# A two-layer hybrid decoder on one core: z chunks between the SSD's halves, SSD groups in three spaced steps, a later norm sum, LRU squares on ScalarE

## The chip, the cores and the metric

The kernel runs on one NeuronCore of a Trainium2 chip. The metric is the device time of one execution in microseconds (us), taken as the median of several runs. The engines are called TensorE (PE in the profile, with PEld for its weight loads), VectorE (DVE), ScalarE (ACT), GpSimd (POOL) and SyncE (SP, which issues nearly all DMAs here).

## The reference, cut to what matters

A trunk of two layers over 256 tokens of width 1024, all in float32. Each layer normalizes and modulates `x`, multiplies it by one wide `w_in`, and feeds three mixers from the product: dilated attention (`q`, `k`, `v`), a Mamba-2 state space mixer (`z`, `xbc`, `dt`; here "SSD"), and a gated linear recurrence ("LRU"). Their outputs are merged under sigmoid gates. A mixture of 32 experts follows.

```python
def mixer_block(h, ...):
    proj = h @ w_in
    q, k, v, z, xbc, dt_raw, lru_gate, lru_x, merge = jnp.split(proj, cuts, axis=-1)
    ...
    y_ssd = ssd_mixer(z, xbc, dt_raw, ...)
    y_lru = rglru_mixer(lru_gate, lru_x, ...)
    merged = g_attn * (y_attn @ w_br_attn) + g_ssd * (y_ssd @ w_br_ssd) + g_lru * (y_lru @ w_br_lru)
    return merged @ w_out

def ssd_mixer(z, xbc, dt_raw, conv_w, conv_b, dt_bias, a_log, d_skip, norm_g):
    xbc = jax.nn.silu(causal_conv(xbc, conv_w, conv_b))
    ...
    y = ssd_chunked(xs * dt[..., None], dt * a, bm, cm)      # 8 groups of 4 heads, 2 chunks of 128 tokens
    y = y + d_skip * xs
    return rmsnorm(y * jax.nn.silu(z), norm_g)

def rglru_mixer(...):
    a = jnp.exp(log_a)
    u = jnp.sqrt(-jnp.expm1(2.0 * log_a)) * (i_gate * xc)
    ...  # h[t] = a[t] h[t-1] + u[t], times gelu(gate_in)
```

## The kernel before

The program is written once in Python as a list of jobs per layer, and a tracing layer adds the semaphores. Within each engine it settles the order when the program is built, by a plan that takes the oldest instruction that the plan holds to be ready; a tile's place is taken from a pool of fixed places and freed behind its last reader. On the chip each engine then works through its own queue in that order.

A layer has a dense part and a MoE part. The dense part is a sequence of jobs, each with several weight loads (mostly 256x512 floats, 512 KB, as one "page" of SBUF). A load passes through `prepare` (ScalarE copies `w` to `wh` in TensorE's rounded format, VectorE or, for every second load, GpSimd makes the rest `wl = w - wh` in line 1451) and, four loads later, through `product` (TensorE, three matmuls of high and low parts for each tile). The chunks of `w_in` come in the order that `_chunks` (line 32) gives: for each half `s` of the SSD `B`, `C`, `X`, `X`; then `v`, four times `q` and `k`, four `z`, the merge gates `m` of branch 1 (the SSD) with that branch's matmuls, the LRU's chunks and gate weights, then merge gates and branches 0 and 2, and the output product. Conditioning jobs (`ada`, short on TensorE) stand between the first chunks: eight in layer 0, four in layer 1.

`chunk_done` takes a finished chunk from PSUM. For `B`, `C` and `X` it runs a convolution (per chunk four ScalarE and twelve VectorE operations) and a Silu; for `z` two ScalarE copies into a page.

All else runs in side threads, Python generators in `Side`. After each load's `product`, `tick` lets up to three due threads go on to their next `yield`; `yield 2` means to go on two ticks later. A thread's instructions thus stand in the program between the dense products. `ssd_groups` (line 865) runs four groups of a half, one every four ticks (`SSD_EVERY`), each with all its instructions in one tick. A group (`ssd_group`) makes `R` (VectorE, the split `av` times the mask `le`), multiplies by `gtr` (TensorE), takes Exp into `L`, forms `cb`, `D` and `E`, and adds the result into `X`. `gate_z` (line 937) waits until all eight groups are done, multiplies `X` by Silu(z), squares on ScalarE, splits the product into `yzh` and `yzl` for branch 1, and adds the squares on GpSimd into `zsum`; the last of the four reduces `zsum` on TensorE into `rz`, the norm factor that `branch_done` (line 1044) applies to branch 1. `attn_pair` (line 788) handles one q and k chunk in four steps, a tick apart. `lru` (line 1006) takes ten tiles of 128x256 one by one (Exp on ScalarE, square on GpSimd, one VectorE operation), two per step, then sqrt, scans and splits by pages.

Pages and loads: `Pages` counts 42 live pages. `Ring.pump` issues further loads on SyncE while fewer than `ahead` are ready and fewer than 42 minus `reserve` pages are live; in the dense part `DENSE = (4, 8)`. Smaller tiles share 11 half pages (`half`).

Lines that are only helpers: 266 every matmul, 274 transposes, 279, 282 and 285 ScalarE's operations, 288, 292 and 297 VectorE's.

Of the kernel before, what the change touches and what calls it, by code (L numbers as in the profile page):

```python
# [17 lines left out]
EPS = 1e-6  # L18
NEG = -1e30
CAP = 64  # L20
SSD_EVERY = 4
N_PAGES, N_HALF = 42, 11

DENSE, BRANCH, OUT, MOE, MOE_END = (4, 8), (99, 9), (99, 3), (99, 4), (99, 18)

# [6 lines left out]
def _chunks():  # L32

    ch = []

    def put(kind, i, c0, n=512):
        ch.append((kind, i, [(c0, c0 + n)]))

    b0, c0 = X0 + 2048, X0 + 3072
    for s in range(2):  # L40
        put("B", s, b0 + 512 * s)
        put("C", s, c0 + 512 * s)
        put("X", 2 * s, X0 + 1024 * s)
        put("X", 2 * s + 1, X0 + 1024 * s + 512)
    for g in range(3):
        put("v", g, V0 + 512 * g)
    for hp in range(4):
        for kind, base in (("q", Q0), ("k", K0)):
            ch.append((kind, hp, [(base + (8 * g + 2 * hp + j) * 64 + 32 * e, base + (8 * g + 2 * hp + j) * 64 + 32 * e + 32)
                                  for e in range(2) for g in range(3) for j in range(2)]))  # L50
    for i in range(4):
        put("z", i, Z0 + 512 * i)
    for n in range(2):
        put("m", (n, 1), MG0 + 1024 + 512 * n)
    put("lx", 0, LX0)
    put("lx", 1, LX0 + 512)
    ch.append(("lxg", 0, [(LX0 + 1024, LX0 + 1280), (LG0, LG0 + 256)]))
    put("lg", 0, LG0 + 256)
    put("lg", 1, LG0 + 768)
    for b in (0, 2):  # L60
        for n in range(2):
            put("m", (n, b), MG0 + 1024 * b + 512 * n)
    return ch
# [64 lines left out]
def bc(ap, shape):  # L128
    return ap.to_broadcast(shape)
# [90 lines left out]
class Trunk:  # L220
# [453 lines left out]
    def layer_start(self, l):  # L674
        self.xbc, self.yT, self.merged, self.rot = {}, {}, {}, {}
        self.lx, self.lg, self.vt = {}, {}, {}
        self.attn_left = 4
        self.ssd_left = 8
        self.dt = None

    def dt_start(self, l, bank):
# [4 lines left out]
    def dt_part(self, l, dT):  # L686
        yield 1
        p = self.ps()
        for b in range(2):
            self.mm(p[:, b * 32:b * 32 + 32], dT[:, b * 128:(b + 1) * 128], self.const("fold"))  # L690
        xin = self.k([128, 74], "sp_x", 1)
        rows = self.rows
        for b in range(2):
            self.tt(xin[:, b * 32:b * 32 + 32], p[:, b * 32:b * 32 + 32], rows[:, 0:32], OP.add)
        self.ts(xin[:, 64:74], self.col(l, "lam"), -1.0, OP.mult)
        sp = self.k([128, 74], "sp_o", 2)
        self.softplus(sp, xin, 74)
        dt = sp[:, 0:64].rearrange("p (b h) -> p b h", b=2)
        self.k8 = self.k([128, 2, 10], "k8", 2)
        self.ts(self.k8[:, 0], sp[:, 64:74], 8.0, OP.mult)  # L700
        self.ts(self.k8[:, 1], sp[:, 64:74], -8.0, OP.mult)
        na = self.k([128, 32], "na", 1)
        self.act(na, rows[:, 32:64], AF.Exp)
        av = self.av = self.k([128, 2, 32], "av", 2)
        for b in range(2):
            self.stt(av[:, b], dt[:, b], -1.0, na, OP.mult, OP.mult)
        self.avh = self.k([128, 2, 32], "avh", 2, F32R)
        self.avl = self.k([128, 2, 32], "avl", 2, F32R)
        self.split_act(self.avh, self.avl, av)
        yield 3  # L710
        p = self.ps()
        self.mm(p[:, 0:32], self.const("gt"), av[:, 0])
        self.dec = self.k([128, 32], "dec", 2)
        self.act(self.dec, p[:, 0:32], AF.Exp)
        self.dt = dt


    def chunk_done(self, job):
# [19 lines left out]
        elif kind == "v":  # L738
            v = self.pages.get([128, 2, 512], F32, "v")
            for b in range(2):  # L740
                self.copy(v[:, b], B[b])
            self.vt[i] = v
        elif kind in ("lx", "lxg", "lg"):
            for t in range(4):
                src = B[t // 2][:, (t % 2) * 256:(t % 2) * 256 + 256]
                if kind == "lx" or (kind == "lxg" and t < 2):
                    ti = 4 * i + t if kind == "lx" else 8 + t
                    if ti % 4 == 0:
                        self.lx[ti // 4] = self.third(ti // 4, "lx")
                    self.conv(self.lx[ti // 4][:, ti % 4], src, self.col(l, "lcw")[:, ti * 4:ti * 4 + 4],  # L750
                              self.col(l, "lcb")[:, ti:ti + 1])
                else:
                    ti = t - 2 if kind == "lxg" else 2 + 4 * i + t
                    if ti % 4 == 0:
                        self.lg[ti // 4] = self.third(ti // 4, "lg")
                    self.copy(self.lg[ti // 4][:, ti % 4], src)
        elif kind == "z":
            z = self.pages.get([128, 4, 256], F32, "z")
            for t in range(2):
                self.copy(z[:, 2 * t:2 * t + 2], B[t])  # L760
            if i == 0:
                self.zT = ([], [])
            self.side.add(self.gate_z(l, i, z))
        elif kind == "m":
            n, b = i
            sg = self.pages.get([128, 2, 512], F32, "sg")
            for t in range(2):
                self.act(sg[:, t], B[t], AF.Sigmoid)
            self.sg = sg
# [17 lines left out]

    def attn_pair(self, l, hp):

        T = {}  # L790
        for kind in "qk":
            T[kind] = self.pages.get([128, 3, 256], F32, kind + "T")
# [39 lines left out]
        for j in range(2):  # L832
            for b in range(2):
                self.ts(P[j][b], P[j][b], den[:, b, j:j + 1], OP.mult)
        yield 1
        if 0 not in self.rot:
            self.rot[0] = (self.pages.get([128, 4, 256], F32R, "yah"), self.pages.get([128, 4, 256], F32R, "yal"))
        py = self.ps()
# [26 lines left out]
    def ssd_groups(self, l, groups):  # L865
# [1 line left out]
        while self.dt is None:  # L867
            yield 1
        for g in groups:
            self.ssd_group(l, g)  # L870
            yield SSD_EVERY
        self.pages.free(2)

    def ssd_group(self, l, g):


        Bt = self.xbc["B", g // 4][:, g % 4]
# [1 line left out]
        X = self.xbc["X", g // 2]  # L879
        xo = 2 * (g % 2)  # L880
        hs = slice(4 * g, 4 * g + 4)
        le = bc(self.const("le")[:, None, :], [128, 4, 128])
        L = self.pages.get([128, 2, 4, 128], F32, "L")
        D = self.pages.get([128, 1024], F32, "D")
        self.nc.vector.memset(L[:, 0, 0, 0:1], 0.0)
        self.nc.vector.memset(D[:, 0:1], 0.0)
        cb = self.half([128, 3, 128], "cb")
        self.nc.vector.memset(cb[:, 0, 0:1], 0.0)
        for c in range(2):
            R = self.pages.get([128, 2, 4, 128], F32R, "R")  # L890
            for i, av in enumerate((self.avh, self.avl)):
                self.tt(R[:, i], bc(av.bitcast(F32)[:, c, hs][:, :, None], [128, 4, 128]), le, OP.mult)
            p = self.ps()
            for i in range(2):
                self.mm(p, self.gtr, R[:, i].rearrange("p h l -> p (h l)"), i == 0, i == 1)
            self.act(L[:, c], p.rearrange("p (h l) -> p h l", h=4), AF.Exp)
            self.pages.free()
        pcb, pxt = self.ps(), self.ps()
        self.mm(pcb[:, 0:256], Bt[:, 0:128], Ct)
        self.mm(pcb[:, 256:384], Bt[:, 128:256], Ct[:, 128:256])  # L900
# [3 lines left out]
        pc = pcb[:, 0:384].rearrange("p (a b) -> p a b", a=3)  # L904
        self.tt(cb[:, 0::2], pc[:, 0::2], bc(self.const("le")[:, None, :], [128, 2, 128]), OP.mult)
        self.copy(cb[:, 1], pc[:, 1])
        xd = D[:, 0:512].rearrange("p (c h d) -> p c h d", c=2, h=4)
        x0 = D[:, 512:768].rearrange("p (h d) -> p h d", h=4)
        E = D[:, 768:1024].rearrange("p (j t) -> p j t", j=2)
# [7 lines left out]
        self.tt(x0, xd[:, 0], bc(self.dec[:, hs][:, :, None], [128, 4, 64]), OP.mult)  # L917
        for c in range(2):
            self.tt(L[:, c], L[:, c], bc(cb[:, 2 * c][:, None, :], [128, 4, 128]), OP.mult)
        pz = self.ps().rearrange("p (j t) -> p j t", j=4)  # L920
        for j in range(2):
            self.mm(pz[:, j], x0[:, 2 * j:2 * j + 2].rearrange("p h d -> p (h d)"), cb[:, 1])
# [9 lines left out]
        xt = X[:, xo:xo + 2, 128:256]  # L932
        self.tt(xt, xt, E, OP.add)
        self.pages.free(2)
        self.ssd_left -= 1

    def gate_z(self, l, i, z):
        while self.ssd_left:
            yield 1
        y = self.xbc["X", i]  # L940
        self.act(z, z, AF.Silu)
# [3 lines left out]
        lo = self.pages.get([128, 4, 256], F32R, "yzl")  # L945
        self.split_act(hi, lo, y)
        if i == 0:
            self.zsum = self.half([128, 2, 256], "zsum")
            self.nc.gpsimd.tensor_tensor(out=self.zsum, in0=z[:, 0:2], in1=z[:, 2:4], op=OP.add)
        else:  # L950
            for h in range(2):
# [3 lines left out]
        hs.append(hi)  # L955
        ls.append(lo)
        if i == 3:
            self.rz = self.k([128, 2], "rz", 2)
            p = self.ps()
            for b in range(2):  # L960
                for t in range(2):
                    self.mm(p[:, b:b + 1], self.zsum[:, t, b * 128:(b + 1) * 128], self.const("ones"), t == 0, t == 1)
            self.rstd(self.rz, p[:, 0:2], 2048)
            self.yT[1] = self.zT


    def third(self, u, name, dtype=F32):
# [38 lines left out]
    def lru(self, l):  # L1006

        sizes = [4, 4, 2]
        rp, ip, tp = self.lr, self.li, self.lt
        for i in range(10):  # L1010
            r, t = rp[i // 4][:, i % 4], tp[i // 4][:, i % 4]
            self.act(r, r, AF.Exp, scale=self.k8[:, 1, i:i + 1])
            sq = self.half([128, 256], "lsq")
            self.nc.gpsimd.tensor_tensor(out=sq, in0=r, in1=r, op=OP.mult)
            self.stt(t, sq, 1.0, t, OP.add, OP.mult)
            if i % 2:
                yield 2
        for u in range(3):
            self.act(tp[u], tp[u], AF.Sqrt)
            self.tt(ip[u], ip[u], tp[u], OP.mult)  # L1020
# [23 lines left out]
    def branch_done(self, job):  # L1044
        l, n, b = job.arg
        B = job.banks
        if n not in self.merged:
            self.merged[n] = self.pages.get([128, 2, 512], F32, "mg")
        mg = self.merged[n]
# [560 lines left out]
```

## Time and profile before

| What | us |
|---|---|
| median of 3 runs | 2315.74 (2311.68 to 2316.73) |
| the profiled execution | 2313.94 |
| its span, first to last instruction | 2312.2 |
| TensorE busy | 2165.8 |
| VectorE busy | 1148.6 |
| ScalarE busy | 798.5 |
| GpSimd busy | 465.5 |

The dense part of layer 0 fills about the first 690 us, its MoE part the time to about 1165, the dense part of layer 1 the time to about 1830, the second MoE part the rest. Matmuls are pipelined, so a busy TensorE isn't one at its peak. The granted clock of TensorE stands at 1.00 (2.4 GHz) or 0.50 (1.2 GHz), and a row shows its mean over a stretch.

### The profile page before, as it was taken

The numbers are of one execution on the slowest core, as the hardware profiler recorded it, in microseconds if no ns is written. First come the engines' busy times: TensorE is split into PE (matmuls) and PEld (weight loads), VectorE is DVE, ScalarE is ACT, GpSimd is POOL, SyncE is SP. The second block draws the span as 40 slices with busy tenths as digits, with TensorE's granted clock in tenths as the row PEclk, the third lists the DMA queues.
The fourth block names the chain that finished last, engine by engine and source line by source line (L and its number), as shares of the span: only waits on it lengthen the run. The fifth ranks groups of instructions, "written<-read, shape, count | busy, mean of one in ns | idle before, by whom it ended". The sixth has DMA issues, their size and how long they took to land. (4 is left out here: it accounts for less than half of the span.)

```text
span 2312.2 us, 32004 instructions
## 1 busy us (share of the span) xinstructions
PE 2165.8 (94%) x12432; PEld 1435.2 (62%) x12432; DVE 1148.6 (50%) x1828; ACT 798.5 (35%) x1234; POOL 465.5 (20%) x209
## 2 busy tenths in 40 slices
PE   6999999999899999999889999999998999999997
PEld 4786888788664444333368878888977544443332
DVE  3878677654752232222167876674485422222222
ACT  3554445536531111011155634473484311111111
POOL 2222334234520000000023332251445000000000
PEclk9999999999999999999999999999999999999998
DMA  9565344574588999999994333347547799999996
GB/s 382 172 219 179 117 137 140 194 256 136 213 347 333 409 409 409 409 409 409 373 346 143 115 107 108 122 159 255 189 157 272 294 409 409 409 409 409 409 409 269
DMA packets 178526, 638.77 MB, mean 276 GB/s; under 512 B 20257, under 2 KB 20513, under 8 KB 178369
## 3 DMA queue, kind: packets, MB, share of 16 engines
q1 hardware_dynamic: 176976, 633.55, 73.5%
q8 instruction: 101, 1.65, 0.3%
q0 software_dynamic: 672, 1.74, 0.2%
q10 hardware_dynamic: 720, 1.37, 0.2%
q14 instruction: 57, 0.46, 0.1%
HBM read 635.53 MB, written 1.05 MB: 275 GB/s over the span
## 5 line engine op out<-in xcount | busy, mean ns | idle before, releaser
L1451 POOL TENSOR_TENSOR wl<-w,wh 128x1024 fp32r<-128x1024 f32 (+1 forms) x159 | 418.5, 2640 | 1250.1 <-ACT wh L285 576.7
L266 PE MATMUL pm<-w,xe 128*64 128x512 f32 x2048 | 502.2, 598 | 14.9 <-DMA w<-in_exp_u_dram 6.7
L266 PEld LDWEIGHTS pm<-w,xe 128*64 128x64 f32 x2048 | 164.6, 137 | 322.3 <-issue 240.4
L285 ACT ACTIVATE wh<-w 128x1024 fp32r<-128x1024 f32 (+1 forms) x316 | 306.1, 1009 | 32.2 <-DMA w<-in_w_in_dram 10.7
L266 PE MATMUL pm<-hh,wh 128*128 128x256 f32 x1056 | 304.8, 289 | 6.0 <-ACT wh L285 3.1
L266 PE MATMUL pm<-hh,wl 128*128 128x256 f32 x1056 | 304.3, 288 | 4.0 <-POOL wl L1451 2.4
L266 PE MATMUL pm<-hl,wh 128*128 128x256 f32 x1056 | 301.6, 286 | 0.0
L1451 DVE TENSOR_TENSOR wl<-w,wh 128x1024 fp32r<-128x1024 f32 (+1 forms) x157 | 271.2, 1732 | 46.1 <-ACT wh L285 41.3
L266 PE MATMUL pm<-w,eaT 128*64 128x512 f32 x1024 | 243.0, 597 | 22.1 <-ACT eaT L285 22.1
L288 DVE TENSOR_TENSOR ea<-ea,pm 128x512 f32<-128x512 f32 x32 | 22.0, 688 | 402.5 <-PE pm L266 402.5
L266 PE MATMUL pm<-wl,hh 128*128 128x512 f32 (+1 forms) x544 | 205.5, 378 | 15.1 <-POOL wl L1451 13.9
L266 PEld LDWEIGHTS pm<-hh,wh 128*128 128x128 f32 x1056 | 204.2, 193 | 21.5 <-ACT wh L285 10.9
L266 PE MATMUL pm<-wh,hh 128*128 128x512 f32 (+1 forms) x544 | 206.0, 379 | 4.4 <-ACT wh L285 2.7
L266 PEld LDWEIGHTS pm<-hh,wl 128*128 128x128 f32 x1056 | 204.3, 194 | 9.0 <-POOL wl L1451 4.0
L266 PEld LDWEIGHTS pm<-hl,wh 128*128 128x128 f32 x1056 | 204.5, 194 | 1.9 <-issue 1.6
L266 PE MATMUL pm<-wh,hl 128*128 128x512 f32 (+1 forms) x544 | 204.4, 376 | 0.0
L266 PEld LDWEIGHTS pm<-w,eaT 128*64 128x64 f32 x1024 | 73.4, 137 | 159.5 <-issue 122.4
L266 PEld LDWEIGHTS pm<-wl,hh 128*128 128x128 f32 x544 | 104.8, 193 | 30.8 <-POOL wl L1451 15.4
L282 ACT ACTIVATE ea<-pm 128x512 f32<-128x512 f32 x32 | 19.1, 597 | 298.0 <-PE pm L266 298.0
L266 PEld LDWEIGHTS pm<-wh,hh 128*128 128x128 f32 x544 | 104.3, 192 | 24.5 <-issue 7.1
L285 ACT ACTIVATE eaT<-pside 128x512 f32<-128x512 f32 x32 | 19.1, 597 | 288.1 <-PE pside L274 288.1
L266 PEld LDWEIGHTS pm<-wh,hl 128*128 128x128 f32 x544 | 105.1, 193 | 13.1 <-issue 1.4
(309 smaller groups left out, 3031.2 us busy)
## 6 DMA issues: line engine op xcount, KB each, us to landing
w<-in_exp_g_dram SPq DMA_DIRECT2D x256, 512.0 KB, 10.2
w<-in_exp_u_dram SPq DMA_DIRECT2D x256, 512.0 KB, 10.2
w<-in_exp_d_dram SPq DMA_DIRECT2D x256, 512.0 KB, 10.2
w<-in_w_in_dram SPq DMA_DIRECT2D x208, 512.0 KB, 4.0
w<-in_ada_w_dram SPq DMA_DIRECT2D x96, 512.0 KB, 5.0
w<-in_w_br_dram SPq DMA_DIRECT2D x60, 512.0 KB, 3.7
w<-in_w_in_dram SPq DMA_DIRECT2D x64, 384.0 KB, 3.1
w<-in_w_out_dram SPq DMA_DIRECT2D x16, 512.0 KB, 4.5
```

Of the source, the lines that this page charges most:

```text
L266: return self.nc.tensor.matmul(o, l, r, start=start, stop=stop, skip_group_check=True)
L282: self.table_op = self.nc.scalar.activation(out=o, in_=i, func=f, **kw).ins
L285: self.nc.scalar.activation(out=o, in_=i, func=AF.Copy)
L288: self.nc.vector.tensor_tensor(out=o, in0=x, in1=y, op=op)
L1451: eng.tensor_tensor(out=lo, in0=w, in1=hi.bitcast(F32), op=OP.subtract)
```

## The change

- `_chunks` puts `z` chunks 0 and 1 behind the first half's `X` chunks, and 2 and 3 behind the second half's.
- A group of the SSD becomes three steps with two ticks between them: both `R` pages; then the products up to `L`, `D` and `cb`; then the last matmuls and the sums. The next group's first step follows the last one in the same tick. The two parts of the split `av` lie in one tile, so that one operation makes a whole `R` page.
- `gate_z` number i waits only for its own two groups. `zsum` has a place of its own, and one half page fewer is there. The last gate hands on its pages first, and reduces `zsum` two ticks later; `branch_done` runs side threads until `rz` is there.
- `attn_pair` starts one tick later and waits one tick more ahead of its last step.
- `lru` squares whole pages on ScalarE instead of tiles on GpSimd, with one VectorE operation per page and three steps in place of five.

```diff
-SSD_EVERY = 4
-N_PAGES, N_HALF = 42, 11
+N_PAGES, N_HALF = 42, 10
...
         put("X", 2 * s + 1, X0 + 1024 * s + 512)
+        for i in (2 * s, 2 * s + 1):
+            put("z", i, Z0 + 512 * i)
...
-    for i in range(4):
-        put("z", i, Z0 + 512 * i)
...
-        self.ssd_left = 8
+        self.ssd_done, self.rz = 0, None
...
-        self.avh = self.k([128, 2, 32], "avh", 2, F32R)
-        self.avl = self.k([128, 2, 32], "avl", 2, F32R)
-        self.split_act(self.avh, self.avl, av)
+        self.avp = self.k([128, 2, 2, 32], "avp", 2, F32R)
+        self.split_act(self.avp[:, 0], self.avp[:, 1], av)
...
+                self.zsum = self.k([128, 2, 256], "zsum", 1)
...
     def attn_pair(self, l, hp):
+        yield 1
...
-        yield 1
+        yield 2
         if 0 not in self.rot:
...
         for g in groups:
-            self.ssd_group(l, g)
-            yield SSD_EVERY
+            yield from self.ssd_group(l, g)
...
-        le = bc(self.const("le")[:, None, :], [128, 4, 128])
+        le = bc(self.const("le")[:, None, None, :], [128, 2, 4, 128])
+        R = []
+        for c in range(2):
+            R.append(self.pages.get([128, 2, 4, 128], F32R, "R"))
+            self.tt(R[c], bc(self.avp.bitcast(F32)[:, :, c, hs][:, :, :, None], [128, 2, 4, 128]), le, OP.mult)
+        yield 2
...
-        for c in range(2):
-            R = self.pages.get([128, 2, 4, 128], F32R, "R")
-            for i, av in enumerate((self.avh, self.avl)):
-                self.tt(R[:, i], bc(av.bitcast(F32)[:, c, hs][:, :, None], [128, 4, 128]), le, OP.mult)
-            p = self.ps()
-            for i in range(2):
-                self.mm(p, self.gtr, R[:, i].rearrange("p h l -> p (h l)"), i == 0, i == 1)
-            self.act(L[:, c], p.rearrange("p (h l) -> p h l", h=4), AF.Exp)
-            self.pages.free()
...
         self.copy(cb[:, 1], pc[:, 1])
+        for c in range(2):
+            p = self.ps()
+            for i in range(2):
+                self.mm(p, self.gtr, R[c][:, i].rearrange("p h l -> p (h l)"), i == 0, i == 1)
+            self.act(L[:, c], p.rearrange("p (h l) -> p h l", h=4), AF.Exp)
+        self.pages.free(2)
...
             self.tt(L[:, c], L[:, c], bc(cb[:, 2 * c][:, None, :], [128, 4, 128]), OP.mult)
+        yield 2
...
-        self.ssd_left -= 1
+        self.ssd_done += 1
...
     def gate_z(self, l, i, z):
-        while self.ssd_left:
+        while self.ssd_done < 2 * i + 2:
             yield 1
...
-            self.zsum = self.half([128, 2, 256], "zsum")
...
         if i == 3:
-            self.rz = self.k([128, 2], "rz", 2)
+            self.yT[1] = self.zT
+            yield 2
+            rz = self.k([128, 2], "rz", 2)
...
-            self.rstd(self.rz, p[:, 0:2], 2048)
-            self.yT[1] = self.zT
+            self.rstd(rz, p[:, 0:2], 2048)
+            self.rz = rz
...
-        for i in range(10):
-            r, t = rp[i // 4][:, i % 4], tp[i // 4][:, i % 4]
-            self.act(r, r, AF.Exp, scale=self.k8[:, 1, i:i + 1])
-            sq = self.half([128, 256], "lsq")
-            self.nc.gpsimd.tensor_tensor(out=sq, in0=r, in1=r, op=OP.mult)
-            self.stt(t, sq, 1.0, t, OP.add, OP.mult)
-            if i % 2:
-                yield 2
+        for u in range(3):
+            for t in range(sizes[u]):
+                i = 4 * u + t
+                self.act(rp[u][:, t], rp[u][:, t], AF.Exp, scale=self.k8[:, 1, i:i + 1])
+            sq = self.third(u, "lsq")
+            self.act(sq, rp[u], AF.Square)
+            self.stt(tp[u], sq, 1.0, tp[u], OP.add, OP.mult)
+            if u < 2:
+                self.pages.free()
+            yield 2
...
     def branch_done(self, job):
         l, n, b = job.arg
         B = job.banks
+        while self.rz is None:
+            self.side.tick(99)
```

## Rows read from the trace of the kernel before

**Rows 1.** The page: busy time by engine, and TensorE's tenths in 40 slices.
```profile
PE 2165.8 (94%) x12432; PEld 1435.2 (62%) x12432; DVE 1148.6 (50%) x1828; ACT 798.5 (35%) x1234; POOL 465.5 (20%) x209
...
PE   6999999999899999999889999999998999999997
```

**Rows 2.** Busy us of the engines by stage; then PE's clock, DMA share, GB/s.
```profile
570.00:580.00 10.00, 10.00 (x46) 8.29 (x45) 9.96 (x9) 6.83 (x10) 8.72 (x6) 1.00 0.45 157
...
1165.00:1830.00 665.00, 626.03 (x3987) 532.40 (x3988) 449.01 (x691) 338.88 (x512) 230.81 (x99) 0.97 0.54 185
1830.00:2312.00 482.00, 449.63 (x2144) 185.12 (x2143) 125.35 (x215) 61.37 (x110) 0.50 (x1) 0.99 0.97 385
```

**Rows 3.** Who TensorE waited for, 420 to 690 us: total, times, longest.
```profile
PE pm L266 <- POOL wl L1451: 6.1, 1, 6.1
PE pm L266 <- ACT wh L285: 1.4, 1, 1.4
```

**Rows 4.** The same over the whole run.
```profile
PE pside L266 <- DVE R L288: 7.9, 7, 2.1
PE pside L266 <- POOL zsum L952: 6.9, 2, 3.5
...
PE pside L266 <- DVE D L288: 4.1, 3, 2.7
PE pside L274 <- DVE rot L288: 4.0, 4, 1.2
...
PE pm L266 <- DVE xbcX L297: 2.6, 2, 1.7
...
PE pside L274 <- DVE Pa L292: 2.4, 6, 0.4
```

**Rows 5.** The stages' columns, for stretches behind a wait.
```profile
413.00:419.50 6.50, 6.50 (x20) 5.44 (x21) 4.35 (x8) 4.73 (x9) 0.00 (x0) 0.50 0.27 83
...
605.50:611.00 5.50, 5.50 (x14) 4.39 (x15) 5.50 (x3) 4.09 (x5) 5.50 (x2) 0.54 0.73 264
...
1337.60:1341.10 3.50, 3.50 (x18) 2.70 (x17) 2.69 (x6) 1.84 (x4) 0.00 (x0) 0.51 0.00 0
...
1741.00:1747.30 6.30, 6.00 (x14) 4.80 (x15) 6.30 (x3) 4.62 (x6) 6.30 (x3) 0.50 0.73 280
```

**Rows 6.** Groups in the LRU, 557.5 to 612 us: busy us, mean ns, idle before.
```profile
L297 DVE SCALAR_TENSOR_TENSOR lt<-lsq,lt 128x256 f32<-128x256 f32 x10 | 11.6, 1200 | 0.5 <-POOL lsq L1014 0.5
...
L1014 POOL TENSOR_TENSOR lsq<-lr 128x256 f32<-128x256 f32 x10 | 8.8, 905 | 1.4 <-ACT lr L282 1.4
```

**Rows 7.** Timeline of the LRU's end: start, us, what, idle before and releaser.
```profile
596.80 1.06 ACT L285 ACTIVATE ylh<-lt 128x1024 fp32r<-128x1024 f32 x1 [6.25 <-DVE lt L288]
...
598.89 13.16 POOL L1451 TENSOR_TENSOR wl<-w,wh 128x1024 fp32r<-128x1024 f32 x3 [13.05 <-ACT wh L285]
```

**Rows 8.** Timeline of VectorE and GpSimd, an SSD group of layer 1.
```profile
1329.99 2.88 DVE L288 TENSOR_TENSOR R<-avh,cn 128x512 fp32r<-128x512 f32 x1
...
1335.57 0.68 DVE L288 TENSOR_TENSOR R<-avh,cn 128x512 fp32r<-128x512 f32 x1
...
1329.76 5.34 POOL L1451 TENSOR_TENSOR wl<-w,wh 128x1024 fp32r<-128x1024 f32 x2 [1.43 <-DVE wl L1451]
```

**Rows 9.** ScalarE's table loads and its Square, groups of 1165 to 1560 us.
```profile
L282 ACT ACT_TABLE_LOAD x13 | 16.7, 1283 | 9.5 <-DVE xbcB L297 3.9 <-DVE acol L297 2.6 <-DVE xbcC L297 2.4
...
L279 ACT ACTIVATE z<-xbcX 128x1024 f32<-128x1024 f32 x4 | 4.2, 1058 | 14.0 <-DVE xbcX L288 14.0
```

**Rows 10.** The gates' sum and product, groups of the same window.
```profile
L952 POOL TENSOR_TENSOR zsum<-zsum,z 128x512 f32<-128x512 f32 x6 | 10.3, 1718 | 8.9 <-ACT z L279 8.7
...
L288 DVE TENSOR_TENSOR xbcX<-xbcX,z 128x1024 f32<-128x1024 f32 x4 | 7.1, 1768 | 1.9 <-ACT z L282 1.9
```

**Rows 11.** Timeline of VectorE ahead of a norm sum.
```profile
1537.14 5.67 DVE L297 SCALAR_TENSOR_TENSOR wl<-w,cols,wh 128x512 fp32r<-128x512 f32 x2
```

**Rows 12.** DMA issues of the page, a q or k chunk's load.
```profile
w<-in_w_in_dram SPq DMA_DIRECT2D x64, 384.0 KB, 3.1
```

## The prediction

> **What bounds the kernel now.** I read the busy shares first. TensorE is busy 2165.8 us of the 2312.2 us span [rows 1], but its digit falls to eight in the 11th and the 31st of 40 slices (578 to 636 and 1734 to 1792 us), near the ends of the two dense parts. The table of stages separates the limits [rows 2]: in a MoE part the DMA share is 0.97 and the rate 385 GB/s, so the experts' weights bind it; in a dense part DMA is at 0.54, VectorE is busy 449 of 665 us, ScalarE 339, GpSimd 231, and TensorE 626. So a dense part is bound by TensorE, and what TensorE waits for there is time. In that table's row of 10 us TensorE is full: 46 matmuls, 0.217 us each; a load of a token chunk is 12 of them, so one tick of the side threads is about 2.6 us there.
>
> A shorter dense part should shorten the whole, one for one. The MoE part that follows is bound by its DMA, and the experts' first pages fill as the dense part frees pages, so its start moves with the dense part's end.
>
> Then I asked who TensorE waits for. Near the end of each dense part stand two waits, 6.1 us for GpSimd's `wl` and 1.4 us for ScalarE's `wh` [rows 3]; both come again in the second layer, 15.0 us in all. Over the whole run there are the SSD's and the attention's waits [rows 4]: the norm sum `zsum` 6.9, `R` 7.9, `D` 4.1, a conv that holds a PSUM bank (`xbcX`) 2.6, `rot` 4.0, `Pa` 2.4.
>
> A wait has a second price. After the `zsum` wait TensorE is full for 6.5 us at a granted clock of 0.50, which is 1.2 of 2.4 GHz; the same follows the LRU wait (0.54 over 5.5 us, 0.50 over 6.3 us) and an `R` wait (0.51 over 3.5 us) [rows 5]. At half clock half of such a stretch is lost. In the LRU: 5.5 x 0.46 + 6.3 x 0.50 = 5.7 us for the two layers. After `zsum`: 3.25 us, and the second layer repeats it, 6.5. In the SSD the stretch occurs twice in layer 1: 3.4.
>
> **Where the waits come from.** In the LRU window VectorE runs ten `lt<-lsq,lt` of 128x256, 11.6 us, and GpSimd ten squares, 8.8 us [rows 6]. ScalarE then stands 6.25 us on the copy `ylh`, whose scan product comes late from VectorE; behind that copy the weight copies `wh` are queued, so GpSimd stands 13.05 us, and then needs 13.16 us for three splits [rows 7]. That is TensorE's 6.1 us.
>
> In the SSD the same shortage shows in small. An `R` product took 0.68 us at 1335.57, but 2.88 us at 1329.99, while GpSimd ran two `wl` splits from 1329.76 for 5.34 us [rows 8]: a VectorE operation with both inputs in SBUF stretches over GpSimd's. The `R` matmul stands right behind its product in the program, so each such 2.2 us reaches TensorE.
>
> **The change part by part.**
>
> *LRU squares.* Removed: ten GpSimd squares (8.8 us) and ten VectorE operations (11.6 us) per layer [rows 6]. Added: three squares on ScalarE; the row of a Square of 128x1024 shows 1.06 us [rows 9], so two of these and one of half the width, about 2.7 us, on an engine with 339 of 665 us busy [rows 2]. VectorE then has three wide operations. The nearest rows are 0.68 us for 512 elements alone and 2.88 us beside GpSimd [rows 8]: two of 1024 and one of 512 are 5 x 0.68 = 3.4 us at best and, with 2.2 us more on each, 10.0 us at worst. I take 4.5, since GpSimd has lost its squares, so VectorE saves 11.6 - 4.5 = 7.1 us (1.6 to 8.2). The thread yields three times by two ticks instead of five times, so the sqrt, the scans and the splits come four ticks earlier, 4 x 2.6 = 10.4 us, while `ylh` was 6.25 us late. The whole of 15.0 + 5.7 = 20.7 us is within reach. ScalarE's order is fixed when the program is built, though, and an operation that VectorE is late for again blocks the `wh` behind it. I take 80%: 16.6 us (0 to 20.7).
>
> *SSD in three steps.* `R` is made two ticks before its matmuls, and `L`, `D`, `cb` two ticks before theirs. Eight groups per layer, as before four ticks apart. The four `R` products of 512 become two of 1024: the same elements, so no gain counted. Two ticks of 2.6 us cover a hit of 2.2 us. In layer 0, where conditioning jobs stand between the chunks, two ticks can be much shorter, but it has little of these waits. The z chunks between the halves carry two ScalarE copies instead of twelve convolution operations on VectorE, so three of the four groups of the first half meet no convolution any more. At stake: `R` 7.9 + `D` 4.1 + `xbcX` 2.6 + clock 3.4 = 18.0 us. I take 70%: 12.6 us (0 to 18.0). Queued behind a late `R` matmul are the dense products, so what is left costs in full.
>
> *z chunks.* Four per layer move; TensorE's matmuls, the weight DMAs on SP's queue and the copies keep their number, so the move itself costs nothing. The gate (Silu, product, square, split, two GpSimd sums) moves from a quiet stretch into the SSD's. Its product took 1.77 us in the mean and its sum 1.72 us [rows 10]. If every second of the eight gates costs one wait of the size of a mean `R` wait, 7.9 / 7 = 1.1 us, that is 4.4 us (0 to 8 x 1.77 = 14). I take 4.
>
> *Later norm sum.* Today TensorE reaches the `zsum` matmuls before GpSimd has added; the cause lies upstream, two VectorE operations that took 5.67 us beside GpSimd [rows 11]. Now two ticks, 5.2 us, are put between, but the chain starts from group 7's matmuls and needs the product, ScalarE's square and two sums of 1.72 us, perhaps 7 us. At stake: 6.9 + 6.5 = 13.4 us; I take half, 6.7 us (0 to 13.4). The consumer, `branch_done`, comes an attention phase later.
>
> *Attention spacing.* One tick before the transposes covers `rot`, one more before the probabilities' transposes covers `Pa`: 6.4 us at stake, 60% taken, 3.8 us (0 to 6.4). No instruction is added. A pair takes five to six ticks of the eight that one q and k chunk give, and the last pair now runs beside the merge chunk and branch 1.
>
> *One half tile fewer, one joint tile for the split of `av`, the wait in `branch_done`:* zero. `zsum` has its own place now and the squares leave the half tiles.
>
> Sum: 16.6 + 12.6 + 6.7 + 3.8 - 4 = 35.7 us. The profiled execution took 2313.9 us, 1.7 more than its span and 1.8 less than the median, so it stands for the runs. 2313.9 - 35.7 = **2278 us**. With every wait gone it would be 2313.9 - 58.5 = 2255.
>
> **Rivals.**
> *The waits move with the work.* The gates fill the room that the z chunks make, and only the LRU part stays: 2313.9 - 16.6 = 2297 us. For it: VectorE is busy 449 us of 665 before and after. Against it: the stretches where it is full are a few, and the change takes convolutions out of them.
>
> *Slower: the page limit.* Through the attention phase the finished gates hold eight split pages where four `X` pages stood. Counted along the program, 29 to 32 pages are live there now; it becomes 33 to 36, and the ring stops to load at 42 - 8 = 34. The four loads that stand ready fall towards none, and a load is asked for only when its split is due. It then needs 3.1 us to land [rows 12], a ScalarE copy of 1.06 us like the one in [rows 7], and a GpSimd split that took 13.16 / 3 = 4.4 us there: 8.6 us, against four ticks ahead of the product, 10.4 us. It decides when that sum passes four ticks. If the 32 loads per layer of the q and k chunks then waited 1 us each, 64 us are lost: 2278 + 64 = 2342. Against it: DMA is at 0.54 there [rows 2], and TensorE's attention work stretches the ticks.
>
> *Function tables on the path.* ScalarE reloads its table thirteen times in layer 1's first 395 us, 1.28 us each [rows 9]. The gates' Silu now stands among the SSD's Exp; two reloads for each of eight gates, all on the path, cost 20.5 us: 2278 + 20.5 = 2299. The Trainium skill, "ScalarE: Activation LUTs", section "Table sets: the hidden batching unit", says to batch calls by table set, which is against this placing; the trace has the reload's price, but no row has a gate among the groups.
>
> *It does not do what it says:* ScalarE's copy `ylh` is placed early again, waits as long, and the SSD's gain is given back by the gates: 2314.
>
> **How the numbers follow.** The forecast, most waits gone, holds 0.58 (2255 to 2292). Waits that move: 0.20. Tables: 0.05. No effect: 0.07. Pages: 0.10. Within 0.2%, 4.6 us, is what a measurement of this kernel cannot tell from no change. So faster 0.83, same 0.07, slower 0.10. The range runs from 2255, all waits gone, to 2309, the upper edge of the moved waits; what is left out above is the no-effect and the page case, 0.17.
>
> **What would show it.** Right: in the wait list `R` and `D` under 3 us each, no 6 us wait for `wl` at the end of the dense parts, ten `lsq` gone from GpSimd, fewer half-clock stretches after the SSD and the LRU. Wrong: `zsum` still 3.5 us per layer; new waits for `wh` or `wl` in the attention phase, released by DMA (pages); `Pb` or `PT` waits beside branch 1.

## The result

The changed kernel takes 2288.6 us, the median of four runs (2287.8 to 2289.5), against 2313.7 us in the runs of before beside them. The ratio is 0.9886, with a 95% interval of 0.9875 to 0.9898: 25 us faster, where 36 were forecast. The range and the sign held. Two terms of the sum did not: the LRU's gave nothing, and the z chunks' had the wrong sign. That the total still came within 11 us of the forecast is in part luck: the other terms gave some 12 us more than forecast and made up for most of the 16.6 us that the LRU did not give.

The page after, to set beside [rows 1]: busy time by engine, and TensorE's tenths in 40 slices.
```profile
span 2286.1 us, 31957 instructions
PE 2155.9 (94%) x12432; PEld 1428.4 (62%) x12432; DVE 1125.2 (49%) x1782; ACT 802.5 (35%) x1240; POOL 440.8 (19%) x189
...
PE   6999999999899999999989999999989999999997
```
The matmuls are the same 12432. GpSimd has 20 instructions fewer (the squares of two layers). The two eights near the ends of the dense parts are still there: those were the slices of the LRU, and nothing was gained in them.

Whom TensorE waited for, over the whole run (total, times, longest), the lines that answer to [rows 4] and those that are new:
```profile
PE pm L265 <- ACT sg L281: 10.1, 4, 5.1
...
PE pm L265 <- ACT wh L284: 6.5, 3, 3.1
...
PE pm L265 <- POOL wl L1459: 5.2, 7, 1.7
PE pside L265 <- ACT cb L284: 5.1, 5, 1.3
PE pm L265 <- DVE wl L1459: 4.4, 3, 2.4
...
PE pside L265 <- POOL zsum L954: 3.6, 2, 1.8
...
PE pside L273 <- DVE Pa L291: 1.9, 5, 0.5
```
`R`, `D` and `rot`, 16 us before, have no line left. `zsum` has halved. The longest wait for GpSimd's `wl` has gone from 6.1 to 1.7 us, but `sg` heads the dense part's waits now, and neither it nor `cb` was a wait before.

**Where the 25 us lie.** Both kernels run the same matmuls, so the start of the k-th matmul in one trace can be set against that in the other. Ahead of layer 0's LRU the changed kernel leads by 6.4 us, behind it by 4.9. Ahead of layer 1's LRU it leads by 30.7, behind it by 29.0, and 25.8 are left at the last matmul. So the LRU stretches lost 1.4 and 1.7 us; the stretches of SSD, norm sum and attention gave some 6 in layer 0 and 24 to 25 in layer 1. Of the lead at the end of layer 1's LRU all but 3 us reached the end of the program.

The stage table for layer 1 from its first matmuls to the LRU, in before and then in after (busy us of PE, PEld, DVE, ACT, POOL, each with its instructions; PE's clock, DMA share, GB/s):
```profile
1163.80:1688.30 524.50, 497.40 (x3402) 432.72 (x3398) 353.79 (x564) 260.56 (x402) 169.32 (x71) 0.98 0.51 167
```
```profile
1158.30:1657.60 499.30, 486.71 (x3402) 425.51 (x3398) 344.50 (x548) 261.47 (x403) 170.32 (x71) 0.99 0.53 176
```
The same 3402 matmuls take 25.2 us less. The waits listed in the two windows, added up, fall from 27.0 to 12.3 us and give 14.7; TensorE's busy time gives the rest, 497.40 - 486.71 = 10.7. Most of that is the clock. These are the stretches at a granted clock of 0.50 in the two windows, first before (to which 1337.60 in [rows 5] belongs), then after:
```profile
1170.40:1177.20 6.80, 5.51 (x26) 5.51 (x27) 3.38 (x6) 2.68 (x7) 1.15 (x1) 0.50 1.02 408
1375.20:1378.60 3.40, 3.40 (x22) 3.07 (x22) 2.45 (x5) 0.84 (x1) 0.00 (x0) 0.50 0.02 5
1487.80:1491.30 3.50, 3.50 (x19) 3.50 (x18) 2.12 (x5) 2.85 (x7) 0.00 (x0) 0.51 0.00 0
1549.30:1556.10 6.80, 6.80 (x20) 5.45 (x20) 4.90 (x8) 5.97 (x10) 0.00 (x0) 0.50 0.24 83
```
```profile
1166.20:1169.60 3.40, 3.33 (x15) 3.33 (x16) 0.92 (x4) 0.15 (x1) 0.00 (x0) 0.50 1.03 411
1401.70:1405.10 3.40, 3.40 (x13) 3.39 (x12) 1.91 (x1) 3.40 (x7) 2.44 (x2) 0.50 0.09 10
```
TensorE is busy 22.7 us at half clock before and 6.7 after. Half of the difference, 8.0 us, is what the clock gave back; the other 2.7 us of busy time stay unexplained. So a us of wait removed brought about half a us more from the clock here.

### The profile page after: what moved, and what is told of

It is laid out like the page before. It is cut to its first block, busy times and chain, and to the rows that moved or that the text cites. A ratio compares the mean times of both kernels' runs of the same rounds, so it can differ in the third digit from the quotient of the medians.

```text
span 2286.1 us, 31957 instructions
## 1 busy us (share of the span) xinstructions
PE 2155.9 (94%) x12432; PEld 1428.4 (62%) x12432; DVE 1125.2 (49%) x1782; ACT 802.5 (35%) x1240; POOL 440.8 (19%) x189
## 4 chain that ended last, share of the span: by engine, by line
PE 36%; DMA 7%; DVE 3%; ACT 2%; issue 2%; POOL 0%; DVEq 0%; SPq 0%; ACTq 0%; POOLq 0%
PE pm L265 29%; PE pside L265 6%; DMA w<-in_exp_u_dram 3%; DMA w<-in_exp_g_dram 3%; PE pside L273 1%; DMA w<-in_exp_d_dram 1%; ACT eaT L284 0%; DVE wl L1459 0%; ACT wh L284 0%; DVE Pb L296 0%; ACT Pb L281 0%; DVE lt L1034 0%; DVE mx L299 0%; ACT Pa L281 0%; DVE xbcX L287 0%
## 5 line engine op out<-in xcount | busy, mean ns | idle before, releaser
L1459 POOL TENSOR_TENSOR wl<-w,wh 128x1024 fp32r<-128x1024 f32 (+1 forms) x159 | 411.1, 2593 | 1234.2 <-ACT wh L284 669.9
L281 ACT ACTIVATE ea<-pm 128x512 f32<-128x512 f32 x32 | 19.1, 597 | 298.2 <-PE pm L265 298.2
L284 ACT ACTIVATE eaT<-pside 128x512 f32<-128x512 f32 x32 | 19.1, 597 | 290.1 <-PE pside L273 290.1
L265 PEld LDWEIGHTS pm<-wh,hl 128*128 128x128 f32 x544 | 103.7, 191 | 12.6 <-issue 0.7
```

The source lines that it names most:

```text
L265: return self.nc.tensor.matmul(o, l, r, start=start, stop=stop, skip_group_check=True)
L281: self.table_op = self.nc.scalar.activation(out=o, in_=i, func=f, **kw).ins
L284: self.nc.scalar.activation(out=o, in_=i, func=AF.Copy)
L1459: eng.tensor_tensor(out=lo, in0=w, in1=hi.bitcast(F32), op=OP.subtract)
```

## The experiments

Times are medians; "after" is the changed kernel, 2288.6 us. The ratio is to the kernel before on the same chip.

**The squares back on GpSimd** (`u_lru`).
```diff
-            sq = self.third(u, "lsq")
-            self.act(sq, rp[u], AF.Square)
-            self.stt(tp[u], sq, 1.0, tp[u], OP.add, OP.mult)
+            sq = self.half([128, 256], "lsq")
+            self.nc.gpsimd.tensor_tensor(out=sq, in0=r, in1=r, op=OP.mult)
+            self.stt(t, sq, 1.0, t, OP.add, OP.mult)
...
+            if i % 2:
+                yield 2
```


> The changed kernel with the LRU's old squares (ten tiles on GpSimd, five steps); everything else as changed. Theory (the LRU part gave nothing: in the changed kernel's trace the lead over the kernel before is 6.4 and 30.7 us ahead of the LRU and 4.9 and 29.0 behind it, since the copy ylh waits in ScalarE's queue as before): 2285.5 us, 3 us faster than the changed kernel, and the waits at the LRU's end back at 7.5 us per layer for wl and wh. Rival (the prediction's sum: the LRU part is worth 16.6 us): 2305 us.

2283.0 us (2280.3 to 2284.2), ratio 0.9868 [0.9853, 0.9883]. The intervals of the ratios overlap with after's, the times of the runs do not, and a second kernel with the old squares (`lru_zsum`, below) gave 2283.3. The waits at the LRU are the old ones, 6.1 us for `wl` and 1.4 for `wh`, and `sg` is gone. So this part of the change is worth nothing, and more likely costs some 5 us. TensorE's waits there add up to 8.0 us per layer, against 8.1 and 8.8 in after: they are not what makes the difference.

**The second yield ahead of the LRU's split** (`fix_lru`).
```diff
             self.tt(tp[u], tp[u], self.lg[u], OP.mult)
+            yield 2
             self.split_act(hi, lo, tp[u])
...
-            yield 2
```


> The changed kernel with the two-tick pause of the LRU's last loop moved ahead of the split, so that the copy ylh and its rest stand two ticks behind the product that they read. Theory (a copy that waits for VectorE blocks the weight copies queued behind it on ScalarE): the waits of 7.7 us per layer at the LRU's end fall below 2 us and the half-clock stretch there goes, some 20 us in all: 2269 us, with ScalarE's idle time ahead of ylh under 2 us. Rival (VectorE is simply full there, so that branch 2 waits for its own operands instead): 2286 to 2290 us, with the wait at another place.

2284.5 us (2283.2 to 2290.0), ratio 0.9881 [0.9866, 0.9897]: no difference from after that can be told. The theory fell: `ylh` is asked for later, yet ScalarE still stood 3.76 and 5.94 us on VectorE's `lt`, and TensorE stood 10.8 us on `sg` at layer 0's LRU, where after has 8.1 in all.

**The LRU's copies on VectorE** (`ylh_dve`).
```diff
-            self.split_act(hi, lo, tp[u])
+            self.nc.vector.tensor_copy(hi, tp[u])
+            self.tt(lo, tp[u], hi.bitcast(F32), OP.subtract)
```


> The changed kernel with the LRU's copies ylh made by VectorE, which makes the product that they read, instead of ScalarE. Theory (a ScalarE copy that waits for VectorE holds up the weight copies and the sigmoids queued behind it): ScalarE's idle time on lt products goes, the waits of 7.7 us per layer for sg, wh and wl at the LRU's end fall under 3 us, and with the half-clock stretch some 15 to 20 us go: 2270 us. Rival (VectorE is full there whatever ScalarE does): 2286 to 2290 us, and TensorE waits for wl of VectorE or for yll in place of sg.

2288.7 us (2287.5 to 2289.3), ratio 0.9892 [0.9877, 0.9907]: no difference, as the rival said; at layer 0's LRU TensorE waits 5.7 us for `sg` and 5.2 for VectorE's `wl`. Freed of the copies, ScalarE's queue stands on the next things that VectorE releases (its timeline: start, us, what, idle before and releaser):
```profile
587.07 1.08 ACT L281 ACTIVATE sg<-pm 128x512 f32<-128x512 f32 x2 [6.14 <-DVE lt L1034]
...
597.18 1.06 ACT L284 ACTIVATE wh<-w 128x1024 fp32r<-128x1024 f32 x1 [6.19 <-DVE wl L1460]
```
This version also puts 3.9 us of copies per layer on VectorE, so it doesn't show what a freed ScalarE would be worth by itself.

**The LRU without its scans** (`no_scan`).
```diff
-            for t in range(sizes[u]):
-                self.nc.vector.tensor_tensor_scan(tp[u][:, t], rp[u][:, t], ip[u][:, t], 0.0, OP.mult, OP.add)
```


> The changed kernel with the ten TENSOR_TENSOR_SCANs of the LRU left out (the recurrence is not computed, so the LRU branch's values are those of its input; everything else is as it was). Theory: TensorE's 7.7 us of gaps at the end of each LRU come from VectorE, which is busy from 571 to 591 us of the span, so that the splits' copies wait on ScalarE for its product lt and the rest of ScalarE's queue behind them. Each scan takes about 0.66 us, 6.6 us per layer: without them the waits on ScalarE's sg (10.1 us) and wh (6.5 us) fall below 5 us together, and the time is about 2279 us (2288.6 less 4 to 5 per layer). Rival: it is ScalarE itself, or the order of its queue, that is late, and the wait only moves once more, as it did in the two other kernels that changed this place: 2286 to 2290 us.

2269.3 us (2266.9 to 2271.6), ratio 0.9805 [0.9788, 0.9821], 19 us under after. Waits at layer 0's LRU, first in after, then here:
```profile
PE pm L265 <- ACT sg L281: 4.7, 2, 4.3
PE pm L265 <- POOL wl L1459: 1.7, 1, 1.7
PE pm L265 <- ACT wh L284: 1.7, 1, 1.7
```
```profile
PE pm L265 <- POOL wl L1457: 1.7, 1, 1.7
PE pm L265 <- ACT sg L281: 0.4, 1, 0.4
```
The stretch 1655 to 1715 us has a granted clock of 1.00 here and 0.91 in after. Against after the k-th matmul gains 8.1 us across layer 0's LRU and 9.3 across layer 1's; 6.1 us of VectorE work per layer (the ten scans) was taken out. Of these gains TensorE's waits give 6.0 us in each layer (8.1 to 2.1, and 8.8 to 2.8); the rest goes with the half clock behind them. The theory was right in direction and in the waits; with 4 to 5 us per layer it had about half of the size. The scans' work and the chain ahead of the copies are shortened together here, and this run can't tell one from the other.

**The SSD group in one tick again** (`u_ssd`).
```diff
-        yield 2
...
-        yield 2
...
+        yield 4
```


> The changed kernel with each SSD group in one tick again (every four ticks); z chunks, gates and joint R as changed. Theory (the steps' spacing removes the waits for R and D): about 8 us slower than the changed kernel, 2297 us, R and D waits together over 5 us. Rival (the z chunks between the halves alone give VectorE the room): R and D waits stay under 2 us, 2288 to 2291 us.

2316.0 us (2310.1 to 2319.5), ratio 1.0006 [0.9996, 1.0015]: the whole gain is gone, 27.4 us. `R` comes back with 6.9 us, `D` with 2.2, `sg` has 13.6 and GpSimd's `wl` 10.9. The theory had the direction and a third of the size. By its trace (2311.1 us) layer 1 ahead of its LRU still gains some 15 us on the kernel before, while layer 0 is 6.2 us behind it: so not all of layer 1's gain is the spacing, and the waits that the theory names are only a part of the cost.

**The SSD steps alone, in the kernel before** (`ssd_alone`). The new `ssd_group` with what it needs; old chunk order, attention, LRU and norm sum.

> The kernel before with the SSD's three spaced steps alone (joint R, gates counted per group, zsum in its own place; z chunks, attention, norm sum and LRU as before). Theory (the spacing carries the gain, as the group in one tick took all 27 us back): 2293 us. Rival (spacing pays only together with the z chunks between the halves, since four groups meet convolutions): 2305 us or more.

2300.5 us (2300.4 to 2305.4), ratio 0.9946 [0.9932, 0.9959], 13 us. By its trace layer 0 loses 5.7 us ahead of its LRU (why was not tried), layer 1 gains 16.4. `R` is gone; `zsum` keeps its 6.9 us, `rot` 4.0, `wl` 15.4. Between the two expectations.

**Three ticks instead of two between the SSD's steps** (`ssd_33`).
```diff
-        yield 2
+        yield 3
...
-        yield 2
+        yield 3
```


> The changed kernel with three ticks instead of two between the three steps of an SSD group. The 27 us that the spacing is worth came with R and D gone from TensorE's waits (6.9 and 4.1 us before, none after). Theory: with two ticks nothing is left to gain there, and what three ticks change is that the SSD ends later: the last z chunks' gates and the norm sum come nearer to the end of the dense part, and the time is 2289 to 2295 us. Rival: the spacing itself keeps paying (fewer stretches at the half clock), and it is under 2284 us.

2301.9 us (2300.3 to 2306.8), ratio 0.9952 [0.9935, 0.9968]: 13 us slower than after. The direction is the theory's; the size is beyond it. Some 8 us go in layer 0 and 8 in layer 1, some is given back later. Why is not settled: `R` and `D` are back with 1.6 and 2.2 us, `wl` from VectorE rises from 4.4 to 7.7, and the norm sum alone (2.2 us a layer) does not carry it.

**The z chunks behind the attention again** (`u_z`).
```diff
-        for i in (2 * s, 2 * s + 1):
-            put("z", i, Z0 + 512 * i)
...
+    for i in range(4):
+        put("z", i, Z0 + 512 * i)
```


> The changed kernel with the four z chunks behind the attention again; spaced groups and all else as changed. Theory (spacing and order both count, since four groups meet convolutions again and the gates with the norm sum stand at the end): about 10 us slower, 2298 us, zsum waiting over 3 us per layer. Rival (spacing alone does it): within 3 us of the changed kernel, 2286 to 2292 us.

2293.2 us (2288.3 to 2294.7), ratio 0.9905 [0.9890, 0.9920]: 4.6 us slower by the medians, at the edge of what can be told, and half of what the theory said. `zsum` is back at 6.8 us.

**Without the two ticks ahead of the norm sum** (`u_zsum`).
```diff
             self.yT[1] = self.zT
-            yield 2
```


> The changed kernel without the two ticks ahead of the norm sum. Theory (the ticks halved the zsum wait from 6.9 to 3.6 us): zsum waits 6 to 8 us again, 4 to 6 us slower, 2294 us. Rival (the plan puts the sum's matmuls where it holds them ready, with or without the ticks): zsum waits 3.6 us as in the changed kernel, 2287 to 2290 us.

2287.5 us (2283.8 to 2291.0), ratio 0.9893 [0.9878, 0.9908]: no difference. `zsum` waits 4.5 us with no pause, 3.6 with it, and 6.8 with the pause but late z chunks (`u_z`). So the halving comes from the order of the z chunks, not from the pause.

**Without the two attention ticks** (`u_attn`).
```diff
-        yield 1
         T = {}
...
-        yield 2
+        yield 1
```


> The changed kernel without the two added ticks of the attention pair. Theory (rot's waits of 4.0 us are gone in the changed kernel, Pa's fell only from 2.4 to 1.9): 2 to 4 us slower than the changed kernel, 2292 us, rot waiting 4 us again. Rival (the waits went with other work that left the attention phase): 2287 to 2290 us, no rot wait.

2297.9 us (2294.1 to 2299.5), ratio 0.9930 [0.9917, 0.9944]: 9.3 us slower, against 2 to 4 in the theory. `rot` is back, with 6.7 us and not 4; layer 0 loses 4.4 us ahead of its LRU. The mean granted clock is 0.986 in its trace and 0.985 in after, so the cost is not one of the clock.

**Two versions built from these.** `lru_zsum` has the edits of `u_lru` and `u_zsum` together.

> The changed kernel with the old LRU squares on GpSimd and without the two ticks ahead of the norm sum, the two edits that alone gave 2283.0 and 2287.5 us against 2288.6. Theory: they add, 2282 us (the pause by itself is within what the measurement can tell). Rival: they share the same wait at the end of the dense part, and it is 2283 to 2286 us.

2283.3 us (2283.0 to 2283.7), ratio 0.9865 [0.9848, 0.9881]: what `u_lru` alone gave. `lru_fix` has the edits of `u_lru` and `fix_lru`.

> The changed kernel with the old LRU squares on GpSimd (alone 2283.0 us) and the LRU's second yield moved ahead of its split (alone 2284.5 us against 2288.6). Theory: with the squares off ScalarE the LRU's end still has GpSimd's split as its last wait (13.8 us in the run); the moved yield lets the scans end before the split's copies are queued on ScalarE, and the time is 2279 us. Rival: the wait is again found at another place of the same stretch, because VectorE's work there is the same: 2282 to 2285 us.

2280.8 us (2279.3 to 2282.4), ratio 0.9855 [0.9839, 0.9872]. Faster than before by 34 us and than after by 8. Its lead over `u_lru` is within both runs' ranges. The waits at the LRU, layer 0, are smaller (first `u_lru`, then this one):
```profile
PE pm L265 <- POOL wl L1457: 6.1, 1, 6.1
PE pm L265 <- ACT wh L284: 1.3, 1, 1.3
PE pm L265 <- DVE wl L1457: 0.6, 1, 0.6
```
```profile
PE pm L265 <- DVE wl L1457: 2.4, 2, 1.9
PE pm L265 <- DVE yll L287: 1.8, 1, 1.8
```
Over the whole run, though, TensorE's wait for the next norm has grown in the same way:
```profile
PE pside L265 <- DVE xnl L296: 5.2, 2, 2.6
```
```profile
PE pside L265 <- DVE xnl L296: 9.6, 2, 5.0
```
A wait for `xnh`, which `u_lru` doesn't have, adds 2.3 us. So the moved yield takes 3.8 us of waiting from layer 0's LRU, and over 3 us per layer come back a little later: most of the wait has moved once more, and a gain in time is not shown.

## Why the forecast held, and where it failed

**LRU squares: 16.6 us forecast, none came.** The parts' costs were near: the squares are gone from GpSimd, ScalarE's cost 2.7 us as worked out, VectorE's three wide operations 6.3 us (4.5 taken, bounds 3.4 to 10.0). So VectorE did save 5.3 us per layer, and the thread did come earlier. These are ScalarE's rows at the LRU's end in after, to set beside [rows 7]:
```profile
579.69 1.06 ACT L284 ACTIVATE ylh<-lt 128x1024 fp32r<-128x1024 f32 x1 [3.50 <-DVE lt L287]
580.65 1.99 ACT L284 ACTIVATE wh<-w 128x1024 fp32r<-128x1024 f32 x2
587.70 1.58 ACT L284 ACTIVATE ylh<-lt 128x512 fp32r<-128x512 f32 x2 [5.05 <-DVE lt L287]
...
592.48 1.08 ACT L281 ACTIVATE sg<-pm 128x512 f32<-128x512 f32 x2
```
The first `ylh` starts 17 us sooner than the one in [rows 7], 11 us of it against TensorE's work, which itself is some 6 us ahead there. Still ScalarE stands 3.50 and 5.05 us on VectorE's product, with `wh` and `sg` queued behind. VectorE in the same stretch (its timeline) has next to no gap:
```profile
571.46 2.95 DVE L287 TENSOR_TENSOR li<-li,lt 128x1024 f32<-128x1024 f32 x3
574.33 1.22 DVE L1459 TENSOR_TENSOR wl<-w,wh 128x1024 fp32r<-128x1024 f32 x1
575.47 3.01 DVE L1034 TENSOR_TENSOR_SCAN lt<-lr,li 128x256 f32<-128x256 f32 x5
578.40 1.19 DVE L287 TENSOR_TENSOR lt<-lt,lg 128x1024 f32<-128x1024 f32 x1
579.52 2.43 DVE L1034 TENSOR_TENSOR_SCAN lt<-lr,li 128x256 f32<-128x256 f32 x4
581.87 3.34 DVE L287 TENSOR_TENSOR yll<-lt,ylh 128x1024 fp32r<-128x1024 f32 x1
585.13 1.21 DVE L287 TENSOR_TENSOR lt<-lt,lg 128x1024 f32<-128x1024 f32 x1
586.26 0.68 DVE L1034 TENSOR_TENSOR_SCAN lt<-lr,li 128x256 f32<-128x256 f32 x1
```
The step that failed is "the sqrt, the scans and the splits come four ticks earlier", set against the 6.25 us by which `ylh` was late. It took the lateness for a matter of the start. The scans are work of VectorE that all the rest stands behind; started earlier by fewer yields, the copies are placed earlier too, and wait as long. The sign that I had named, no 6 us wait for `wl`, came true and was worth nothing, since the wait now stands under `sg`. I had named this outcome as a rival ("`ylh` is placed early again, waits as long") and took 20% off the term for it; it was all of it. `ylh_dve` and `fix_lru` show that moving the wait on ScalarE's queue does not end it, `no_scan` that taking the scans out of the stretch does: 6.1 us per layer were worth 8 to 9 us.

Why the 5.3 us that VectorE saved were worth nothing shows in its timeline ahead of that stretch, in after:
```profile
556.02 1.23 DVE L296 SCALAR_TENSOR_TENSOR lt<-lsq,lt 128x1024 f32<-128x1024 f32 x1 [1.80 <-ACT lsq L278]
...
560.87 2.19 DVE L296 SCALAR_TENSOR_TENSOR lt<-lsq,lt 128x1024 f32<-128x1024 f32 x1 [1.87 <-ACT lsq L278]
...
564.11 2.86 DVE L296 SCALAR_TENSOR_TENSOR lt<-lsq,lt 128x512 f32<-128x512 f32 x1
```
They were saved at the thread's front, where VectorE now stands idle for ScalarE's squares; the scans, products and splits behind it are the same work as before. One rival is left untested: the `yll` of 3.34 us, which takes 1.22 us elsewhere, stretches beside a GpSimd split and so makes some 2 of ScalarE's 5.05 us. No run took that split away.

**SSD in three steps: 12.6 us forecast.** Alone in the old kernel it measured 13 us, near the forecast, though as a gain of 16.4 in layer 1 less a loss of 5.7 in layer 0 that I had not foreseen: that the sum fits is in part luck. Taken out of the new one it costs 27.4. The mechanism is the one given, as far as `R` and `D` go: 12.0 us of waits before, none in after, 9.1 in `u_ssd`. VectorE and GpSimd beside each other in layer 1, after, to set beside [rows 8]:
```profile
1323.36 1.22 DVE L287 TENSOR_TENSOR R<-avp,cn 128x1024 fp32r<-128x1024 f32 x1
...
1325.27 2.65 DVE L287 TENSOR_TENSOR R<-avp,cn 128x1024 fp32r<-128x1024 f32 x1
```
```profile
1323.43 3.41 POOL L1459 TENSOR_TENSOR wl<-w,wh 128x1024 fp32r<-128x1024 f32 x1 [3.31 <-DVE xbcX L296]
```
The first `R` began 0.07 us ahead of the split and took 1.22 us; the split took 3.41 us where 2.4 is usual, and the second `R`, issued into it, 2.65 us. Nobody waited for it: the two ticks cover the hit.

**z chunks: -4 forecast, about +4.6 measured.** The product in layer 1 took 1.23 us in the mean (1.77 in [rows 10]), and none of the eight gates' operations stands in TensorE's list except the sum. Other waits are longer than in `u_z`: `cb`, a copy on ScalarE, 5.1 us against 3.0, and VectorE's `wl` 4.4 against 1.3, together 5.2 us, near the 4 that I took. That the gates cause them is not shown. What the step left out is what the new order gives: an earlier norm sum, which I had put down to the pause (3.6 against 6.8 us), and shorter waits for `xbcX` and `Pa`.

**Norm sum: 6.7 forecast.** The wait fell from 6.9 to 3.6 us; the half taken was right, but the pause had no share that can be measured.

**Attention: 3.8 forecast, 9.3 measured** by taking it out. The term was mis-sized: in the new kernel the two ticks cover 6.7 us of `rot`, not the 4.0 of before, and `Pb` with 0.9, which I had not counted.

The three together with the gates were put at 19.1 us and gave about 31 (24 to 25 of them in layer 1). Two things were too low: the shares taken of each stake, and the clock. Of the waits named as at stake, layer 1 had 18.6 us ahead of its LRU, and 2.7 are left. Of its clock I had named 3.4 + 3.25 = 6.7 us; 5.1 of these came back, and 2.9 more behind waits whose clock I had not counted (`Pb` at 1487.80, and the layer's first matmuls, which the change doesn't touch). The parts are also not a sum. Taken out one at a time they cost 27.4 + 9.3 + 4.6 = 41 us, more than all of them gave. The likely reason, argued and not shown, is that each one removed brings back waits that the others had covered too.

**The rivals.** The waits that move with the work came true in the one place where I had excepted them, the LRU. The page limit did not show: of layer 1's waits ahead of the LRU (dg 4.0, `cb` 2.8, `zsum` 1.8, `xbcC` 1.2, `yel` 1.0, `Pa` 0.9, `wl` 0.6 us) none was released by a DMA. Function tables, over the whole run before and after:
```profile
L282 ACT ACT_TABLE_LOAD x49 | 62.9, 1283 | 21.8 <-DVE xbcB L297 6.8 <-DVE xbcC L297 4.7 <-DVE xbcX L297 3.7
L281 ACT ACT_TABLE_LOAD x49 | 62.9, 1283 | 14.6 <-DVE xbcB L296 4.3 <-issue 3.4 <-DVE xbcX L296 2.8
```
The count and the time are the same (49, 62.9 us). The rule of the Trainium skill, "ScalarE: Activation LUTs", section "Table sets: the hidden batching unit", to batch calls by table set, was not broken further by this placing. No run here shows what more loads would have cost.

## What to carry over

A producer that is late because its engine is full was not helped here by an earlier start or by another queue for the consumer. Look whether the engine has idle time in the very stretch; if it has none, work taken off it there counts (the scans), while work taken off ahead of it only became idle time (the squares). Look also where else a wait comes back before calling it gone. Price a wait of TensorE with the clock behind it: here about half a us on each us of wait. And where several edits cover the same waits, measure each in the old kernel and out of the new one, since the two answers differ (13 and 27 us here).

## What was not expected of the hardware

Scans stretch beside GpSimd's splits as other VectorE operations do. In before, at layer 0's LRU, a group of three of 128x256 that ran beside a split took 4.05 us and one of four without a split 2.43 us; five took 3.01 us in after with no split beside them, and 5.18 in `ylh_dve` with one. Either engine can lose. In after the `yll` of 3.34 us began 0.1 us behind a GpSimd split, which kept its 2.35 us. In `u_lru` two splits that began beside running VectorE operations took 9.82 us:
```profile
581.77 2.35 POOL L1459 TENSOR_TENSOR wl<-w,wh 128x1024 fp32r<-128x1024 f32 x1 [11.38 <-ACT wh L284]
```
```profile
592.74 9.82 POOL L1457 TENSOR_TENSOR wl<-w,wh 128x1024 fp32r<-128x1024 f32 x2 [13.05 <-ACT wh L284]
```
The Trainium skill, "SBUF — State Buffer", section "Who interferes with whom", says that a VectorE operation with two SBUF inputs and a GpSimd operation that reads SBUF exclude each other, and that the one that issues first holds the port while the other blocks. The first row agrees with it: the split, issued first, kept its time, and `yll` ended 1.1 us behind the split's end, about what it takes alone. In the second, GpSimd loses to several VectorE operations in a row: the four from 592.88 to 596.43 us keep their usual times (1.22, 0.68, 0.68 and 1.22 us) while the first split is under way.
